# Gate and up projections of two feature blocks at a time: seven products of quarters in place of eight

## The chip, the cores and the metric

The kernel runs on one core of a Trainium2 chip, in one launch. The metric is the device time of that launch in microseconds (us), lower is better. The engines are named as the profile names them: PE (TensorE, matmuls; PEld is its weight load), DVE (VectorE), ACT (ScalarE), POOL (GpSimd) and SP (SyncE, which issues the DMAs here).

## The reference, cut to what matters

A first block, then two layers, each a mixer of four branches followed by a feed-forward part; 512 tokens of width 1024 in float32. Only the feed-forward part of the two layers is changed:

```python
D_MODEL, SEQ, D_FF = 1024, 512, 2816

def hybrid_layer(x, ...):                 # twice, on 512 x 1024
    ...                                   # four branches, merged by gates
    x = x + merged.astype(dt) @ w_out
    h2 = rms_norm(x, norm2_g)
    ffn = (jax.nn.silu(h2 @ w_ffn_gate) * (h2 @ w_ffn_up)) @ w_ffn_down
    return x + ffn
```

## The kernel before

**Split numbers.** Every float32 operand of a matmul is kept as two tiles, a high part (`hi`, a cast on ACT) and the rest (`lo`, a subtraction on POOL, in some places on DVE). One product is three matmuls into the same PSUM bank, high by high, high by low and low by high (`mm3`, lines 246 to 250), each with its own load of 128x128 weights.

**Feed-forward part.** The 2816 features are 22 blocks of 128. `act` holds the normalised tokens, transposed: 8 tiles of 128 features by 512 tokens, `hi` and `lo`. `block` computes one feature block: `proj_t` (line 252) takes the 8 weight tiles of gate, splits them four at a time (`split_w`, line 215: 128x512, cast on ACT at line 220, low part on POOL at line 222, three buffers for each part), and runs 8 x 3 matmuls of 512 columns; `silu2` (line 350) follows, then the same for up, the product (line 1067) and its two parts `yh` and `yl`. `down` multiplies two finished blocks by their rows of `w_ffn_down` (`proj_n`, lines 296 to 298) and adds the result to `x` (`add_resid`, line 497). It runs one block behind, so PE always has work whose operands are there. The last four blocks have no `down` of their own: `proj_resid` (line 543) takes their weights ahead, split into the buffers `pth`, `ptl` and `ks`, and finishes the token tiles one by one, each followed by its norm.

**Edges.** Before the feed-forward part `proj_resid` multiplies by `w_out_2`; per token tile `norm_tile` (line 523) normalises, transposes on PE and splits into `act`. The last of these steps are handed on in `k.late` and run inside the first gate projection, half of the tokens at a time (`proj_late`, lines 267 to 279).

**Order.** PE runs in the order in which the program is written; the other engines' instructions are ordered by a scheduler at build time, each queue then runs strictly in order. Waits between engines come from the tiles: a tile's buffer is given again when its last reader is through. Weight loads go through three buffers `raw` of 128x1024 (512 KB each). `t2` has six buffers, `p` four, PSUM eight banks.

Of the kernel before, what the change touches and what calls it, by code (L numbers as in the profile page):

```python
# [18 lines left out]
P = 128  # L19
S = 512  # L20
# [47 lines left out]
class Task:  # L68
    def __init__(self, gen, cost):
        self.gen, self.left, self.done = gen, cost, False  # L70
# [89 lines left out]
def pe_cost(n):  # L160
    return max(n / 2.4 + 3, 110)
# [3 lines left out]
def hybrid_kernel(ctx: ExitStack, tc: tile.TileContext, i: dict, out: bass.AP):  # L165
# [77 lines left out]

    def mm3(ps, sh, sl, mh, ml, first, last):

        T_.matmul(ps, sh, mh, start=first, stop=False)  # L248
        T_.matmul(ps, sh, ml, start=False, stop=False)  # L249
        T_.matmul(ps, sl, mh, start=False, stop=last)  # L250

    def proj_t(outs, raw, nk):

# [284 lines left out]
    def proj_resid(get, ap, k0, nk, on_tile, delay=1):  # L538

        pss = [[bank(), bank()] for _ in range(NT)]  # L540
        for kk in range(nk - 4):
# [479 lines left out]
def hybrid_layer(k, spill, h, l, last):  # L1021
# [19 lines left out]
    def on_tile(t, pss):  # L1041
        for half, ps in enumerate(pss):
            k.add_resid(x, t, half, ps, ss)
        return k.norm_tile(x[:, t], t, ss, act, gain)

    k.proj_resid(lambda kk, t: tuple(a[:, kk, t * P:(t + 1) * P] for a in act), i["w_out_2"][l], 0, KD, on_tile)
    return ffn(k, x, l, act, last)


def ffn(k, x, l, h, last):  # L1050
    nc, i, new, V, A_, f, pool, bank, stream = k.nc, k.i, k.new, k.V, k.A_, k.f, k.pool, k.bank, k.stream
    gw, uw = (k.w_cols(i[n][l]) for n in ("t_gate", "t_up"))
    wd = i["w_ffn_down_2"][l]

    def get(kk):
        return h[0][:, kk], h[1][:, kk]

    def block(last=False):
        pg = bank()
        for _ in k.proj_t([(pg, get)], next(gw), KD):  # L1060
            pass
        gt = k.silu2(pg, k.t2())
        pu = bank()
        for _ in k.proj_t([(pu, get)], next(uw), KD):
            pass
        pr = k.t2()
        V.scalar_tensor_tensor(pr, pu, 0.5, gt, ALU.mult, ALU.mult)  # L1067
        hi, lo = k.y_tile()
        A_.copy(hi, pr)
        (V if last else k.G).tensor_tensor(lo, pr, f(hi), ALU.subtract)  # L1070
        return hi, lo

    def down(a, acts):
        for half in range(2):
# [18 lines left out]
    ss = new(k.small, [P, 8], "xss")  # L1093
# [16 lines left out]
    k.proj_resid(lambda kk, t: tuple(b[:, t * P:(t + 1) * P] for b in acts[kk]), wd, KF - 4, 4, on_tile)  # L1110
    return (None, None) if last else (spill, h)


# [743 lines left out]
```

## Time and profile before

| | |
|---|---|
| median of 3 runs | 2634.25 us (2632.74 to 2640.15) |
| profiled execution | 2637.59 us, span 2635.8 us |
| mean granted TensorE clock | 0.989 |
| PE busy | 2554.8 us, 97% |
| DVE, ACT, POOL busy | 1334.6, 1162.8, 1291.5 us (51%, 44%, 49%) |

The span runs from the first instruction of the program to the last; the 1.8 us between it and the time of the same execution lie around it. Busy times of different engines overlap, and a matmul counts as busy until its modelled end, so neighbouring matmuls overlap as well. The granted clock is 1.00 at the full 2.4 GHz and 0.50 at 1.2.

### The profile page before, as it was taken

The numbers are of one execution on the slowest core, as the hardware profiler recorded it, in microseconds if no ns is written. First come the engines' busy times: TensorE is split into PE (matmuls) and PEld (weight loads), VectorE is DVE, ScalarE is ACT, GpSimd is POOL, SyncE is SP. The second block draws the span as 40 slices with busy tenths as digits, with TensorE's granted clock in tenths as the row PEclk, the third lists the DMA queues.
The fourth block names the chain that finished last, engine by engine and source line by source line (L and its number), as shares of the span: only waits on it lengthen the run. The fifth ranks groups of instructions, "written<-read, shape, count | busy, mean of one in ns | idle before, by whom it ended". The sixth has DMA issues, their size and how long they took to land.

```text
span 2635.8 us, 36300 instructions
## 1 busy us (share of the span) xinstructions
PE 2554.8 (97%) x12918; PEld 2127.0 (81%) x12918; DVE 1334.6 (51%) x2895; ACT 1162.8 (44%) x2533; POOL 1291.5 (49%) x1112
## 2 busy tenths in 40 slices
PE   7999989999999999999999999999999999999998
PEld 7878778778887887788888887888888877888887
DVE  3677547858536466432222368685364573322223
ACT  4567645436534445332222454365454453322223
POOL 3443345442465543545555555524655535455554
PEclk9999999999999999999999999999999999999999
DMA  4542232222436332422222332223364233222222
GB/s 144 143 130 69 82 125 97 70 77 72 135 112 180 114 104 81 144 81 96 96 96 96 109 110 69 83 73 103 122 182 127 94 91 139 85 96 96 96 96 88
DMA packets 117732, 276.96 MB, mean 105 GB/s; under 512 B 15824, under 2 KB 37584, under 8 KB 117552
## 3 DMA queue, kind: packets, MB, share of 16 engines
q1 hardware_dynamic: 117552, 274.65, 33.2%
q8 instruction: 102, 1.67, 0.3%
q14 instruction: 78, 0.64, 0.1%
HBM read 230.26 MB, written 6.46 MB: 90 GB/s over the span
## 4 chain that ended last, share of the span: by engine, by line
PE 75%; DVE 10%; POOL 4%; issue 4%; DMA 3%; ACT 2%; SPq 0%; POOLq 0%; DVEq 0%; ACTq 0%
PE A L248 17%; PE A L249 16%; PE A L250 16%; PE A L296 5%; PE A L297 5%; PE A L298 5%; PE A L314 4%; PE A L443 3%; POOL wlo L222 2%; DMA raw<-in_w_out_dram 1%; DVE ptl L211 1%; DMA cb<-in_c_rpb_z_dram 1%; PE A L488 1%; DVE sm L331 1%; PE A L278 1%
## 5 line engine op out<-in xcount | busy, mean ns | idle before, releaser
L222 POOL TENSOR_TENSOR wlo<-raw,whi 128x512 fp32r<-128x512 f32 (+2 forms) x721 | 926.7, 1288 | 903.1 <-ACT whi L220 894.8
L220 ACT CAST whi<-raw 128x512 fp32r<-128x512 f32 (+2 forms) x733 | 443.9, 608 | 777.6 <-PE A L249 447.4
L248 PE MATMUL A<-hi,whi 128*128 128x512 f32 (+1 forms) x1848 | 744.3, 403 | 0.4 <-ACT hi L210 0.4
L250 PE MATMUL A<-hi,wlo 128*128 128x512 f32 (+1 forms) x1848 | 725.7, 393 | 10.3 <-DVE wlo L222 5.8
L249 PE MATMUL A<-lo,whi 128*128 128x512 f32 (+1 forms) x1848 | 727.0, 393 | 0.4 <-DVE lo L211 0.4
L250 PEld LDWEIGHTS A<-hi,wlo 128*128 128x128 f32 x1848 | 349.7, 189 | 91.0 <-DVE wlo L222 7.5
L248 PEld LDWEIGHTS A<-hi,whi 128*128 128x128 f32 x1848 | 350.4, 190 | 66.2 <-ACT whi L220 0.9
L249 PEld LDWEIGHTS A<-lo,whi 128*128 128x128 f32 x1848 | 350.3, 190 | 64.2 <-DVE lo L211 0.6
L314 PE MATMUL A<-ident,p 128*128 128x128 f32 (+3 forms) x1125 | 175.5, 278 | 28.1 <-DVE p L527 19.9
L497 DVE TENSOR_TENSOR x<-x,A 128x512 f32<-128x512 f32 x176 | 120.0, 688 | 154.0 <-PE A L298 96.8
L314 PEld LDWEIGHTS A<-ident,p 128*128 128x128 f32 (+3 forms) x1125 | 135.7, 139 | 67.2 <-DVE p L527 19.1
L211 DVE TENSOR_TENSOR ptl<-A,pth 128x512 fp32r<-128x512 f32 (+3 forms) x256 | 148.9, 583 | 80.0 <-ACT pth L210 78.9
L332 ACT ACTIVATE p<-p,sm 128x512 f32<-128x512 f32 (+6 forms) x160 | 100.7, 629 | 155.2 <-DVE sm L331 154.0
L354 DVE SCALAR_TENSOR_TENSOR t<-t,A 128x512 f32<-128x512 f32 x44 | 30.3, 688 | 252.7 <-ACT t L353 252.7
L210 ACT CAST pth<-A 128x512 fp32r<-128x512 f32 (+3 forms) x256 | 127.5, 502 | 54.6 <-PE A L314 54.2
L310 POOL TENSOR_TENSOR rstd<-rstd,mhalf 128x1 f32<-128x1 f32 (+2 forms) x80 | 56.0, 701 | 194.4 <-DVE rstd L309 187.8
L296 PE MATMUL A<-whi,hi 128*128 128x256 f32 (+7 forms) x440 | 145.9, 332 | 0.0
L297 PE MATMUL A<-wlo,hi 128*128 128x256 f32 (+7 forms) x440 | 143.1, 325 | 1.1 <-POOL wlo L222 1.1
L298 PE MATMUL A<-whi,lo 128*128 128x256 f32 (+7 forms) x440 | 142.9, 325 | 0.0
L1067 DVE SCALAR_TENSOR_TENSOR t<-A,t 128x512 f32<-128x512 f32 x44 | 30.4, 692 | 171.2 <-PE A L250 171.2
L296 PE MATMUL A<-whi,yh 128*128 128x512 f32 x288 | 112.1, 389 | 0.0
L297 PE MATMUL A<-wlo,yh 128*128 128x512 f32 x288 | 112.1, 389 | 0.0
(365 smaller groups left out, 4563.3 us busy)
## 6 DMA issues: line engine op xcount, KB each, us to landing
raw<-in_t_gl_dram SPq DMA_DIRECT2D x64, 512.0 KB, 3.5
raw<-in_t_gate_dram SPq DMA_DIRECT2D x44, 512.0 KB, 3.4
raw<-in_t_up_dram SPq DMA_DIRECT2D x44, 512.0 KB, 3.4
raw<-in_w_ffn_down_dram SPq DMA_DIRECT2D x44, 512.0 KB, 3.7
raw<-in_w_in_dram SPq DMA_DIRECT2D x26, 512.0 KB, 3.5
raw<-in_w_out_dram SPq DMA_DIRECT2D x24, 512.0 KB, 3.5
ks<-sth SPq DMA_DIRECT2D x64, 128.0 KB, 2.4
ks<-stl SPq DMA_DIRECT2D x64, 128.0 KB, 2.4
```

The lines of the kernel that those rows point to most:

```text
L210: A_.copy(hi, ps)
L211: V.tensor_tensor(lo, ps, f(hi), ALU.subtract)
L220: A_.copy(hi, src)
L222: (V if k.lo and k.turn % k.lo == 0 else G).tensor_tensor(lo, src, f(hi), ALU.subtract)
L248: T_.matmul(ps, sh, mh, start=first, stop=False)
L249: T_.matmul(ps, sh, ml, start=False, stop=False)
L250: T_.matmul(ps, sl, mh, start=False, stop=last)
L296: T_.matmul(ps, sh, wh[:, j], start=(b + j == 0), stop=False)
L297: T_.matmul(ps, sh, wl[:, j], start=False, stop=False)
L298: T_.matmul(ps, sl, wh[:, j], start=False, stop=(b + j == nk - 1))
L314: T_.transpose(dst, src, ident[0:k, 0:k])
L497: V.tensor_tensor(xx, xx, ps, ALU.add)
```

## The change

Two feature blocks are computed at a time. The 1024 x 256 weights of the two blocks are four quarters (512 features of the input by 128 output features each: a11, a12 of the first block, a21, a22 of the second), the tokens are four quarters too (512 features by 256 tokens: b11, b12, b21, b22), and the result is four quarters of 128 by 256. In place of eight products of quarters, seven are formed, from sums of quarters (Strassen's scheme in Winograd's form). The sums of the weights, s1 to s4, are made per call of `fast_pair`; those of the tokens, t1 to t4, once per layer by `Tokens.sums`, from float32 copies of the token quarters that `norm_tile` now writes as well. Every sum is split into high and low part as other operands are. A product is 12 matmuls of 256 columns. Three of the seven accumulate onto a bank that was read before (`first=False`). The first gate pair of a layer is computed as before (`plain`). `silu2` of the gates and the products with up now read their operand from SBUF (`dst`) in place of PSUM. `down` always takes two blocks and follows a whole pair; the last four blocks go to `proj_resid`, whose odd weight tiles have new homes.

```diff
-    def mm3(ps, sh, sl, mh, ml, first, last):
+    def mm3(ps, sh, sl, mh, ml, first, last, **kw):
...
-    def norm_tile(x, t, ss, dst, gain):
+    def norm_tile(x, t, ss, dst, gain, quarters=None):
...
-                evict_split(ps.rearrange("p (j c) -> p j c", j=4), *(d[:, 4 * half:4 * half + 4, t * P:(t + 1) * P] for d in dst))
+                src = ps.rearrange("p (j c) -> p j c", j=4)
+                evict_split(src, *(d[:, 4 * half:4 * half + 4, t * P:(t + 1) * P] for d in dst))
+                if quarters:
+                    A_.copy(quarters[half][t // 2][:, :, (t % 2) * P:(t % 2 + 1) * P], src)
...
+    class Tokens:
...
+        def sums(self):
+
+            (b11, b12), (b21, b22) = self.q
+            hi = new(pool, [P, 4, 4, 256], "v", F32R, 1)
+            lo = [new(pool, [P, 2, 4, 256], "ks", F32R) for _ in range(2)]
+            self.t = [(hi[:, j], lo[j // 2][:, j % 2]) for j in range(4)]
+            for c in (slice(0, 2), slice(2, 4)):
+                t = [t2().rearrange("p (k c) -> p k c", k=2) for _ in range(4)]
+                V.tensor_tensor(t[0], b12[:, c], b11[:, c], ALU.subtract)
+                V.tensor_tensor(t[1], b22[:, c], t[0], ALU.subtract)
+                G.tensor_tensor(t[2], b22[:, c], b12[:, c], ALU.subtract)
+                V.tensor_tensor(t[3], b21[:, c], t[1], ALU.subtract)
+                for j in (1, 2, 0, 3):
+                    A_.copy(self.t[j][0][:, c], t[j])
+                    (G if j % 2 else V).tensor_tensor(self.t[j][1][:, c], t[j], f(self.t[j][0][:, c]), ALU.subtract)
...
+    def fast_pair(raw1, raw2, tok, dst):
+
+        a11, a12, a21, a22 = raw1[:, 0:4], raw1[:, 4:8], raw2[:, 0:4], raw2[:, 4:8]
...
+        def split(src, eng):
+            hi, lo = (new(pool, [P, 512], t, F32R, 3).rearrange("p (k c) -> p k c", k=4) for t in ("whi", "wlo"))
+            A_.copy(hi, src)
+            eng.tensor_tensor(lo, src, f(hi), ALU.subtract)
+            return hi, lo
+
+        s1, s2, s3, s4 = (part() for _ in range(4))
+        h1, l1 = (new(pool, [P, 4, 256], n, F32R).rearrange("p a b -> p (a b)").rearrange("p (k c) -> p k c", k=KD) for n in ("pth", "ptl"))
+        A_.copy(h1, raw1)
+        G.tensor_tensor(l1, raw1, f(h1), ALU.subtract)
+        V.tensor_tensor(s1, a21, a22, ALU.add)
+        V.tensor_tensor(s2, s1, a11, ALU.subtract)
+        w6 = split(s2, V)
+        V.tensor_tensor(s3, a11, a21, ALU.subtract)
+        w7 = split(s3, G)
+        w5 = split(s1, V)
+        V.tensor_tensor(s4, a12, s2, ALU.subtract)
+        t1, t2_, t3, t4 = tok.t
+        pa, pd, pb, pc = (bank()[:, 0:256] for _ in range(4))
+
+        def product(ps, w, m, first=True):
+
+            for j in range(4):
+                mm3(ps, w[0][:, j], w[1][:, j], m[0][:, j], m[1][:, j], first and j == 0, j == 3, skip_group_check=not first)
+            return 12 * pe_cost(256)
+
+        u, (d1, d2) = t2(), dst
+        q, u2 = u[:, 0:256], u[:, 256:512]
+        yield product(pa, (h1[:, 0:4], l1[:, 0:4]), tok.quarter(0, 0))
+        A_.copy(q, pa)
+        yield product(pd, w6, t2_)
+        V.tensor_tensor(u2, q, pd, ALU.add)
+        yield product(pb, w7, t3)
+        V.tensor_tensor(q, u2, pb, ALU.add)
+        yield product(pc, w5, t1)
+        V.tensor_tensor(d2[:, 256:512], q, pc, ALU.add)
+        yield product(pa, (h1[:, 4:8], l1[:, 4:8]), tok.quarter(1, 0), False)
+        A_.copy(d1[:, 0:256], pa)
+        yield product(pb, split(a22, G), t4, False)
+        V.tensor_tensor(d2[:, 0:256], u2, pb, ALU.add)
+        yield product(pc, split(s4, V), tok.quarter(1, 1), False)
+        V.tensor_tensor(d1[:, 256:512], u2, pc, ALU.add)
+
+    def proj_resid(get, ap, k0, nk, on_tile, delay=1, home=None):
...
-            if kk % 2:
+            if home and kk % 2:
+                wh, wl = home()
+            elif kk % 2:
...
-    def block(last=False):
-        pg = bank()
-        for _ in k.proj_t([(pg, get)], next(gw), KD):
+    def plain(w):
+        ps = bank()
+        for _ in k.proj_t([(ps, get)], next(w), KD):
             pass
...
+    def pair(first, last):
+
+        if first:
+
+            gts = [k.silu2(plain(gw), k.t2()) for _ in range(2)]
+            tok.sums()
+        else:
+            gts = [k.silu2(g, k.t2()) for g in fast(gw)]
+        out = []
+        for u, gt in zip(fast(uw), gts):
+            V.scalar_tensor_tensor(gt, u, 0.5, gt, ALU.mult, ALU.mult)
+            hi, lo = k.y_tile()
+            A_.copy(hi, gt)
+            (V if last else k.G).tensor_tensor(lo, gt, f(hi), ALU.subtract)
+            out.append((hi, lo))
+        return out
...
-    for a, n in [(a, 2) for a in range(0, KF - 4, 2)] + [(KF - 4, 4)]:
-        acts = []
-        for j in range(n):
-            acts.append(block(j == 3))
-            if pending:
-                down(*pending)
-                pending = None
+    for a in range(0, KF, 2):
+        acts = pair(a == 0, a == KF - 2)
+        if a == KF - 2:
+            acts = pending[1] + acts
+        elif pending:
+            down(*pending)
         pending = (a, acts)
```

## Rows read from the trace of the kernel before

**Rows 1.** The page, part 1: busy us, share of span, instructions.

```profile
PE 2554.8 (97%) x12918; PEld 2127.0 (81%) x12918; DVE 1334.6 (51%) x2895; ACT 1162.8 (44%) x2533; POOL 1291.5 (49%) x1112
```

**Rows 2.** The page, part 4: chain that ended last, by line.

```profile
PE A L248 17%; PE A L249 16%; PE A L250 16%; PE A L296 5%; PE A L297 5%; PE A L298 5%; PE A L314 4%; PE A L443 3%; POOL wlo L222 2%; DMA raw<-in_w_out_dram 1%; DVE ptl L211 1%; DMA cb<-in_c_rpb_z_dram 1%; PE A L488 1%; DVE sm L331 1%; PE A L278 1%
```

**Rows 3.** Windows, both layers: us, busy PE PEld DVE ACT POOL, clock, DMA.

```profile
1200.00:1300.00 100.00, 100.00 (x436) 81.55 (x436) 24.95 (x37) 29.33 (x49) 54.33 (x43) 1.00 0.28 95
...
2400.00:2500.00 100.00, 100.00 (x436) 81.55 (x435) 25.19 (x38) 29.08 (x48) 54.65 (x43) 1.00 0.28 95
```

**Rows 4.** Timeline of PE, first layer: start us, us, engine, line, operation.

```profile
1160.70 0.40 PE L248 MATMUL A<-hi,whi 128*128 128x512 f32 x1
...
1163.48 0.40 PE L296 MATMUL A<-whi,yh 128*128 128x512 f32 x1
...
1174.38 0.40 PE L248 MATMUL A<-hi,whi 128*128 128x512 f32 x1
```

**Rows 5.** Timeline of PE: first and last of 96 matmuls, 256 columns.

```profile
396.70 0.28 PE L296 MATMUL A<-whi,hi 128*128 128x256 f32 x1
...
407.90 0.28 PE L298 MATMUL A<-whi,lo 128*128 128x256 f32 x1
```

**Rows 6.** Groups: PEld 396:408, POOL and ACT 1200:1300 (busy, mean ns | idle).

```profile
L296 PEld LDWEIGHTS A<-whi,hi 128*128 128x128 f32 x32 | 6.0, 188 | 0.0
...
L222 POOL TENSOR_TENSOR wlo<-raw,whi 128x512 fp32r<-128x512 f32 x37 | 47.9, 1294 | 45.8 <-ACT whi L220 45.8
L220 ACT CAST whi<-raw 128x512 fp32r<-128x512 f32 x37 | 23.0, 621 | 69.7 <-PE A L249 45.3 <-PE A L298 24.4
```

**Rows 7.** Groups by line and form, DVE, whole span.

```profile
L497 DVE TENSOR_TENSOR x<-x,A 128x512 f32<-128x512 f32 x176 | 120.0, 688 | 154.0 <-PE A L298 96.8 <-PE A L250 57.2
...
L211 DVE TENSOR_TENSOR v<-A,v 128x256 fp32r<-128x256 f32 x24 | 9.2, 417 | 4.0 <-ACT v L210 3.9
...
L1468 DVE TENSOR_TENSOR t<-t,t 128x512 f32<-128x512 f32 x10 | 6.9, 688 | 0.2
```

**Rows 8.** Groups by form: POOL and ACT at 256 columns, whole span.

```profile
L1631 POOL TENSOR_TENSOR cb<-cb,cst 128x256 f32<-128x256 f32 x32 | 24.2, 762 | 29.0 <-DMA cb<-in_c_rpb_z_dram 22.1 <-PE A L250 2.6 <-DVE ptl L211 1.8
...
L210 ACT CAST v<-A 128x256 fp32r<-128x256 f32 x24 | 8.5, 373 | 3.3 <-PE A L298 3.0
```

**Rows 9.** Timeline: a DVE operation behind a POOL operation.

```profile
1060.88 1.29 POOL L222 TENSOR_TENSOR wlo<-raw,whi 128x512 fp32r<-128x512 f32 x1 [1.45 <-ACT whi L220]
...
1061.07 1.64 DVE L1152 TENSOR_TENSOR x<-x,t 128x512 f32<-128x512 f32 x1
```

**Rows 10.** Timeline of DVE and POOL: the same at 547 us.

```profile
547.34 1.29 POOL L222 TENSOR_TENSOR wlo<-raw,whi 128x512 fp32r<-128x512 f32 x1
...
547.40 1.77 DVE L1463 TENSOR_TENSOR t<-t,rstd 128x512 f32<-128x512 f32 x1 [1.76 <-POOL rstd L310]
```

**Rows 11.** Timeline of ACT, feed-forward part of the first layer.

```profile
1144.05 0.62 ACT L220 CAST whi<-raw 128x512 fp32r<-128x512 f32 x1 [1.26 <-PE A L249]
...
1147.35 0.59 ACT L353 ACTIVATE t<-A 128x512 f32<-128x512 f32 x1
```

**Rows 12.** Timeline, start of that part: ACT's last casts, PE's next matmul.

```profile
1132.13 1.31 ACT L210 CAST hi<-A 128x512 fp32r<-128x512 f32 x2 [2.63 <-PE A L314]
...
1135.69 0.39 PE L248 MATMUL A<-hi,whi 128*128 128x512 f32 x1
```

**Rows 13.** Timeline of PE behind idle; that window, columns as in rows 3.

```profile
537.05 0.33 PE L314 MATMUL A<-ident,yn 128*128 128x128 f32 x1 [1.75 <-DVE yn L1384]
...
537.75 0.42 PE L297 MATMUL A<-wlo,hi 128*128 128x256 f32 x1
...
540.74 0.41 PE L296 MATMUL A<-whi,hi 128*128 128x256 f32 x1
...
537.00:541.00 4.00, 3.95 (x21) 3.95 (x22) 1.04 (x2) 1.50 (x3) 2.10 (x2) 0.58 0.02 4
```

**Rows 14.** The page, part 6: DMA issues, KB each, us to landing.

```profile
raw<-in_t_gate_dram SPq DMA_DIRECT2D x44, 512.0 KB, 3.4
```

More of the change, by code (lines that the diff above doesn't have):

```diff
@@ L242, in w_cols @@
                 yield raw[:, m]
-    def mm3(ps, sh, sl, mh, ml, first, last):
-        T_.matmul(ps, sh, mh, start=first, stop=False)
-        T_.matmul(ps, sh, ml, start=False, stop=False)
-        T_.matmul(ps, sl, mh, start=False, stop=last)
+    def mm3(ps, sh, sl, mh, ml, first, last, **kw):
+        T_.matmul(ps, sh, mh, start=first, stop=False, **kw)
+        T_.matmul(ps, sh, ml, start=False, stop=False, **kw)
+        T_.matmul(ps, sl, mh, start=False, stop=last, **kw)
     def proj_t(outs, raw, nk):
@@ new lines, in norm_tile, with __init__, quarter @@
+        return second
+    class Tokens:
+        def __init__(self, h, quarters):
+            self.h, self.q = h, quarters
+        def sums(self):
[12 more added lines that the diff above has]
+                    (G if j % 2 else V).tensor_tensor(self.t[j][1][:, c], t[j], f(self.t[j][0][:, c]), ALU.subtract)
+        def quarter(self, a, b):
+            return tuple(z[:, 4 * a:4 * a + 4, 256 * b:256 * b + 256] for z in self.h)
@@ new lines, in fast_pair, with part @@
+    def fast_pair(raw1, raw2, tok, dst):
+        a11, a12, a21, a22 = raw1[:, 0:4], raw1[:, 4:8], raw2[:, 0:4], raw2[:, 4:8]
+        def part():
+            return p_tile().rearrange("p (k c) -> p k c", k=4)
+        def split(src, eng):
[36 more added lines that the diff above has]
+        V.tensor_tensor(d1[:, 256:512], u2, pc, ALU.add)
@@ L1043, in on_tile, with ffn @@
             k.add_resid(x, t, half, ps, ss)
-        return k.norm_tile(x[:, t], t, ss, act, gain)
+        return k.norm_tile(x[:, t], t, ss, act, gain, quarters)
+    quarters = [[a.rearrange("p a b -> p (a b)")[:, 0:1024].rearrange("p (k c) -> p k c", k=4) for a in z]
+                for z in ([k.q_stack().bitcast(F32) for _ in range(2)], [new(k.mix, [P, 2, S], "cst", bufs=2) for _ in range(2)])]
     k.proj_resid(lambda kk, t: tuple(a[:, kk, t * P:(t + 1) * P] for a in act), i["w_out_2"][l], 0, KD, on_tile)
-    return ffn(k, x, l, act, last)
-def ffn(k, x, l, h, last):
+    return ffn(k, x, l, act, quarters, last)
+def ffn(k, x, l, h, quarters, last):
     nc, i, new, V, A_, f, pool, bank, stream = k.nc, k.i, k.new, k.V, k.A_, k.f, k.pool, k.bank, k.stream
     gw, uw = (k.w_cols(i[n][l]) for n in ("t_gate", "t_up"))
+    tok = k.Tokens(h, quarters)
     wd = i["w_ffn_down_2"][l]
@@ L1056, in get, with fast @@
         return h[0][:, kk], h[1][:, kk]
-    def block(last=False):
-        pg = bank()
-        for _ in k.proj_t([(pg, get)], next(gw), KD):
-            pass
-        gt = k.silu2(pg, k.t2())
-        pu = bank()
-        for _ in k.proj_t([(pu, get)], next(uw), KD):
-            pass
[L1066 to L1071, printed above, removed]
+    def plain(w):
+        ps = bank()
+        for _ in k.proj_t([(ps, get)], next(w), KD):
+            pass
+        return ps
+    def fast(w):
+        dst = [k.t2() for _ in range(2)]
+        for _ in k.fast_pair(next(w), next(w), tok, dst):
+            pass
+        return dst
+    def pair(first, last):
[12 more added lines that the diff above has]
+        return out
     def down(a, acts):
@@ L1108, in on_tile, with home @@
             nc.sync.dma_start(k.out[t * P:(t + 1) * P, sl], x[:, t, sl])
-    k.proj_resid(lambda kk, t: tuple(b[:, t * P:(t + 1) * P] for b in acts[kk]), wd, KF - 4, 4, on_tile)
+    homes = iter(((pool, "qs"), (k.mix, "cst")))
+    def home():
+        where, tag = next(homes)
+        return tuple(new(where, [P, 1024], tag, F32R, 2) for _ in range(2))
+    k.proj_resid(lambda kk, t: tuple(b[:, t * P:(t + 1) * P] for b in acts[kk]), wd, KF - 4, 4, on_tile, home=home)
     return (None, None) if last else (spill, h)
```

1 line of the change is left out of this document (removed).

## Prediction

> **What bounds the kernel now.** I read the page first: TensorE (PE) is busy 97% of the span, no other engine above 51% [rows 1], and the largest lines of the chain that ended last are the three matmuls of `mm3`, 49% of the span together [rows 2]. A busy PE only means that matmuls overlap, so the feed-forward part needs a closer look. Windows of 100 us inside that part show PE busy throughout at full granted clock, 436 matmuls each, DVE at 25, ACT at 29 and POOL at 54 [rows 3]. The four that lie there, two in each layer, agree: the stage has no stall, and only fewer or shorter matmuls shorten it. The timeline gives the spacing: 12 projection matmuls of 512 columns from 1160.70 to 1163.48 us, 231.7 ns each; 48 of the down projection from there to 1174.38, 227.1 ns each [rows 4]. Two feature blocks of gate or up are 48 matmuls, 11.12 us.
>
> **The change, term by term.** `fast_pair` stands for 48 matmuls of 512 columns and issues 7 products x 12 = 84 of 256 columns, each with its own weight load. Is half the width half the time? In 396 to 408 us the trace has 96 such matmuls in a row, a fresh weight load for each: 396.70 to 407.90 in 95 steps, 117.9 ns [rows 5]. A load lasts 188 ns [rows 6], longer than that step, so loads overlap each other too, and the weights do not become the limit. One call is 84 x 0.1179 = 9.90 us against 11.12: 1.22 us saved. The first gate pair of a layer stays plain, so a layer has 11 pairs x 2 - 1 = 21 calls, two layers 42: **-51.1 us**. The down projection keeps its 24 matmuls per block.
>
> What is added goes to the other engines. Per call: DVE seven 128x512 operations with both inputs in SBUF (s1 to s4, three low parts) and five 256-column additions from PSUM; ACT a 1024-column cast, five of 512 and two 256-column copies out of PSUM; POOL the 1024-column low part of raw1 (`l1`) and two of 512 (w7, a22). Prices are 0.69 and 0.42 us on DVE [rows 7], 0.62 and 0.37 on ACT, 1.29 on POOL for 512 columns [rows 6, 8]. No row has POOL at 1024; from 0.76 at 256 columns [rows 8] to 1.29 at 512 the slope is 0.53 per 256, so 2.36 (lower bound one 512 operation, 1.29; upper two, 2.58; a line through two rows is nearer to the upper). PE needs 2 x 9.90 + 48 x 0.2271 = 30.7 us for a pair (gate, up, down). In that time ACT has 2 x (7 x 0.62 + 2 x 0.37) for the calls and 8 x 0.62 beside (tanh, `yh`, down splits), 15 us. DVE has 14 x 0.69 + 10 x 0.42 + four more with two SBUF inputs (the two of `silu2`, whose source now lies in SBUF, and the two products of gate and up) x 0.69 + 8 additions to x at 0.69 = 22 us. POOL has 2 x (2.36 + 2 x 1.29) + 2 `yl` and 4 down splits at 1.29 = 17.6 us. By that count all is hidden.
>
> But DVE and POOL do not run freely beside each other. An addition on DVE with both inputs in SBUF took 1.64 us where a POOL operation had begun 0.19 us before: POOL ended at 1062.17, DVE at 1062.71 [rows 9]. Another took 1.77 and again ended 0.54 us after a POOL operation that had begun first (549.17 against 548.63) [rows 10]; undisturbed ones take 0.69 [rows 7]. So they take turns, and DVE holds its turn for 0.54. (The Trainium skill, SBUF — State Buffer, section Who interferes with whom, has this as a lock on a shared port pair, held for the whole instruction against a DVE operation with two SBUF inputs; the trace agrees, with the 0.54 us above. Free overlap, the first sum, would give 2587; under the lock the added work has to queue.) DVE additions with one PSUM input stay at 0.69 while POOL works in 54 of 100 us [rows 3, 7] and do not queue. Turns in one pair: POOL 17.6, DVE 18 x 0.54 = 9.7, together 27.3 of 30.7 us. That is 89% full, and PE waits whenever a low part comes late.
>
> How late? The split pool keeps its three buffers. The fourth split of a call (a22) takes the buffer of the first (w6), free when product 2 ends; its low part is wanted by the third matmul of product 6, 3 x 1.415 + 0.24 = 4.48 us on. Cast 0.62 and POOL 1.29 leave 2.6, less some 0.4 of hand-overs: 2.2 us of slack. w7 and the first two down splits have about the same; the low parts made on DVE 2.8. If `l1` (2.36) has just begun and a DVE turn (0.54) comes between, a22 starts 2.90 late and PE stands 0.70 us. Each call has one `l1` and two such splits; with the worst meeting about half the time I take 0.35 per call, **+14.7 us**. Bounds: 0, if nothing meets, and 2.0 (another POOL operation of 1.29 in front as well), +84. The value is nearer to 0 since today POOL waits for ACT and ACT for PE in this stage, never PE for them [rows 3, 6].
>
> Does the text's order matter? In `fast_pair` the cast of a22 stands behind the copy of pa, which waits for product 5, and DVE's low part of s4 behind an addition that waits for product 6. If the queues kept that order, PE would wait 0.37 + 0.62 + 1.29 and 0.42 + 0.69, 3.4 us per call. They do not: at 1144.05 ACT casts weights of up, and only at 1147.35 comes the tanh of the gate, which is written ahead of them [rows 11]. PE alone follows the text. I cost this at nothing.
>
> Edges of the stage, per layer. (a) `norm_tile` adds two 128x512 ACT copies between casts that PE waits for, at 1132.13 to 1133.44 us [rows 12]: 0.4 (0 to 1.1). (b) `Tokens.sums` can start when these casts and copies are through, about 1134.5. It has 6 POOL and 10 DVE turns: 6 x 1.29 + 10 x 0.54 = 13.1. With the last gate split, w7 and a22 (3.9) and the low parts of w6 and w5 (1.1) the turns are taken until 1152.6. PE ends the plain gates at 1135.69 [rows 12] + 24 x 0.2317 = 1141.2 and wants a22 and t4 five products later, at 1148.3. That is 4.3 late; I take 4.0, some of it being movable ahead (0 to 6). (c) The last pair has no down projection beside it, and the eight splits of the tail (10.3 of POOL) fall on it: two calls 17.4, `silu2` and products 2.2, low parts 1.1, altogether 31 of turns against 23.9 of PE until the last of them is wanted (two calls and 18 matmuls), of which some 4.5 (one `l1` and four sums) can go ahead: 2.5 (0 to 5). (d) Where PE stands long its clock halves: after 1.75 us of idle the clock granted over 537 to 541 was 0.58, and 256-column matmuls went from 0.118 to 0.214 us a step (14 steps from 537.75 to 540.74), 1.4 us lost [rows 13]. One such stretch per layer and a little over, 1.7 (0 to 3.4). Together 8.6 x 2 = **+17.2 us**.
>
> Costed at nothing: PSUM reuse (pa, pb and pc are written again two or three products, 2.8 us, after the read of 0.42 begins; without that cover 0.42 per product); weight traffic (the same 512 KB loads, 3.4 us to landing [rows 14], six in 30.7 us through three buffers; on SP's queue the two loads of down stand behind those of up and the next gate's behind them, so if raw2, held until a22 is split, came free a pair late, 3.4 us once per pair).
>
> **Sum.** 2637.6 (the profiled execution) - 51.1 + 14.7 + 17.2 = 2618.4. The median of the runs shown is 3.3 lower, so **2615 us**.
>
> **Rivals.** *All hidden*: the turns interleave and PE stays at 100%: 2637.6 - 51.1 + 1 = 2587, 2584 on the median's scale. For it: 11% of the time no turn is taken and the order adapts. Against: two splits per call with 2.2 us of slack, and an operation of 2.36 that they can meet. *The turns eat it*, the change doing nothing for the time: at 0.81 us of waiting per call ((51.1 - 17.2) / 42) the gain is gone; waits of 0.65 to 1.0 give 2627 to 2642. It comes so if time is lost at each hand-over; DVE ending 0.54 after POOL, no later than its own work needs, speaks against much loss [rows 9, 10]. *Slower*: queues settled beforehand on undisturbed durations put DVE's sums for the next call ahead of low parts that PE needs; from 0.81 us per call on the kernel is slower, and at the upper bound of 2.0 it takes 2637.6 - 51.1 + 84 + 17.2 = 2688. For it: DVE would be at 72% before any waiting. Against: every product leaves at least 2.2 us. That 256-column matmuls fall back to 131 ns or more, where 84 cost as much as 48 now, is excluded by [rows 5] unless the clock falls.
>
> **Numbers.** My forecast (2597 to 2626) 0.42, all hidden 0.20, eaten 0.18, slower 0.20. A change under 0.3% (8 us) can't be told from none. Faster 0.62, same 0.18, slower 0.20. The range, 2588 to 2652, leaves out the best part of all hidden and the worst half of slower.
>
> **What the profile after should show.** Some 84 x 42 matmuls of 256 columns at 118 ns start to start where PE does not wait; PE busy below 100% in the middle of the feed-forward part, its idle time in front of `wlo` matmuls and released by POOL; DVE operations with two SBUF inputs above 0.69 us in the mean, one with PSUM unchanged; PE waits of a few us where the up products of the first pair begin, and some at the tail. Wrong would be: no PE waits at all (then 2584), waits on PSUM additions or on DMA, or half clock through the stage.

## The result and the profile after

The changed kernel takes **2742.5 us** (median of 4 runs, 2737.7 to 2752.5) against 2635.2 for the kernel before: ratio **1.041** (95% interval 1.038 to 1.044). It is slower by 107 us, far outside the predicted range. The profiled execution took 2742.57 us with a span of 2740.8, 105.0 longer than before's.

First the page, part 1, of the kernel after, to be held against [rows 1], then windows over the two feed-forward stages (from the last `proj_late` of a layer to the next, or to the end) of before and of after, columns as in [rows 3].

```profile
PE 2553.2 (93%) x14430; PEld 2194.7 (80%) x14430; DVE 1705.8 (62%) x3421; ACT 1269.7 (46%) x2733; POOL 1333.8 (49%) x1080
```

```profile
1128.00:1499.30 371.30, 369.83 (x1643) 301.83 (x1641) 97.26 (x150) 115.54 (x201) 199.42 (x157) 1.00 0.29 99
2260.90:2628.40 367.50, 366.95 (x1619) 299.42 (x1617) 95.30 (x146) 111.73 (x193) 195.07 (x154) 1.00 0.28 95
```

```profile
1131.70:1554.00 422.30, 368.08 (x2400) 335.72 (x2397) 283.20 (x413) 165.41 (x296) 218.55 (x141) 0.95 0.27 87
2317.30:2733.80 416.50, 365.83 (x2375) 332.57 (x2373) 282.07 (x409) 162.12 (x288) 215.03 (x138) 0.95 0.27 84
```

Read the two pairs from left to right. The stages grew by 51.0 and 49.0 us, 100 of the 105: nothing else moved much. PE, which had next to no idle time there (1.5 and 0.5 us), now has 54.2 and 50.7 (length less busy time): 102.9 more. PE's busy time hardly fell, although its matmuls are shorter; the clock column says why. At a mean of 0.95 some 5% of 838.8 us, 42, was lost to the lower clock. What is left, 100.0 - 102.9 - 42 = -45 us, is the saving: by this remainder it came, near the predicted 51. Waiting and the lower clock around the waits took it three times over.

What PE waited for in the whole span (us in total, times, longest), largest first:

```profile
PE A L250 <- POOL wlo L580: 53.9, 20, 3.1
...
PE A L297 <- POOL wlo L222: 18.7, 20, 1.9
PE A L248 <- ACT v L564: 18.2, 4, 5.4
```

L250 is the third matmul of `mm3`, L580 the low part inside `split`. Twenty waits are one for each of the 20 gate calls that `fast_pair` makes, 2.7 us each. L564 is the cast of the token sums, at the start of each stage. One pair, in the middle of layer 0, shows how the long wait arises. PE at the wait (start, length, [idle before]), and then the clock of the stretches around it (windows, columns as above):

```profile
1319.08 0.39 PE L250 MATMUL A<-v,wlo 128*128 128x256 f32 x1 [2.88 <-POOL wlo L580]
...
1320.43 0.41 PE L248 MATMUL A<-v,whi 128*128 128x256 f32 x1
...
1323.63 0.30 PE L248 MATMUL A<-hi,pth 128*128 128x256 f32 x1
```

```profile
1319.00:1320.00 1.00, 0.93 (x7) 0.93 (x8) 0.91 (x2) 0.00 (x0) 1.00 (x2) 1.00 0.00 0
1320.50:1323.50 3.00, 3.00 (x16) 3.00 (x16) 2.86 (x6) 1.06 (x2) 0.22 (x1) 0.50 0.40 149
```

This wait costs 2.88 us and then once more: from 1320.5 to 1323.5 the granted clock is 0.50, the 1.2 GHz level, and a step of 256 columns takes 0.21 us (15 from 1320.43 to 1323.63) in place of 0.118. Not every wait is paid twice like this one: of the 20, 12 came with such a stretch, and 38 of the 85 us at half clock lie at the two starts and at the end of layer 0. Now backwards from the wait: POOL, ACT, DVE and SP's DMA issues before it (each a timeline, the last the line's own view: first and last start).

```profile
1314.94 2.39 POOL L586 TENSOR_TENSOR ptl<-raw,pth 128x1024 fp32r<-128x1024 f32 x1 [4.66 <-ACT pth L585]
1317.28 1.75 POOL L580 TENSOR_TENSOR wlo<-p,whi 128x512 fp32r<-128x512 f32 x1
```

```profile
1312.22 0.62 ACT L579 CAST whi<-p 128x512 fp32r<-128x512 f32 x1 [6.84 <-DVE p L588]
1313.81 1.05 ACT L585 CAST pth<-raw 128x1024 fp32r<-128x1024 f32 x1 [0.97 <-DMA raw<-in_t_up_dram]
```

```profile
1308.41 0.71 DVE L587 TENSOR_TENSOR p<-raw 128x512 f32<-128x512 f32 x1 [4.71 <-DMA raw<-in_t_gate_dram]
1309.05 2.47 DVE L497 TENSOR_TENSOR x<-x,A 128x512 f32<-128x512 f32 x4
1311.44 0.68 DVE L588 TENSOR_TENSOR p<-p,raw 128x512 f32<-128x512 f32 x1
```

```profile
L240 SPq DMA_DIRECT2D raw<-in_t_gate_dram x2: 340/340/340, 1296.0 to 1304.9; - x2
```

The gate call's first load is issued at 1296.0, its second only at 1304.9: it had to wait for one of the three raw buffers, which the down projection's splits give back. So `s1` (L587) starts at 1308.41, four additions into x stand between it and `s2` (L588), and the first cast is made at 1312.22. Then the queues: ACT casts `h1` of the *up* call (L585) before the gate's w7, and POOL makes `l1` of the up call (L586, 2.39 us) before w7's low part, which PE is waiting for. Three candidate causes lie in one picture: late weights, the fixed order of the queues, and the turns of DVE and POOL (the 1.75 us of the low part, 1.29 undisturbed [rows 6]).

### The profile page after: what moved, and what is told of

Same layout as the page of the kernel before. It is cut to its first block, busy times and chain, and to the rows that moved or that the text cites. A ratio compares the mean times of both kernels' runs of the same rounds, so it can differ in the third digit from the quotient of the medians.

```text
span 2740.8 us, 40242 instructions
## 1 busy us (share of the span) xinstructions
PE 2553.2 (93%) x14430; PEld 2194.7 (80%) x14430; DVE 1705.8 (62%) x3421; ACT 1269.7 (46%) x2733; POOL 1333.8 (49%) x1080
## 4 chain that ended last, share of the span: by engine, by line
PE 55%; DVE 12%; POOL 12%; DMA 9%; issue 8%; ACT 4%; SPq 0%; POOLq 0%; DVEq 0%; ACTq 0%
PE A L250 12%; PE A L248 12%; PE A L249 12%; POOL wlo L222 4%; PE A L314 4%; DMA raw<-in_t_gate_dram 4%; PE A L443 3%; PE A L297 2%; PE A L296 2%; PE A L298 2%; POOL wlo L580 2%; DMA raw<-in_t_up_dram 2%; POOL ptl L586 1%; POOL yl L1170 1%; DMA raw<-in_w_out_dram 1%
## 5 line engine op out<-in xcount | busy, mean ns | idle before, releaser
L222 POOL TENSOR_TENSOR wlo<-raw,whi 128x512 fp32r<-128x512 f32 (+4 forms) x553 | 718.5, 1304 | 643.1 <-ACT whi L220 637.9
L248 PE MATMUL A<-hi,whi 128*128 128x512 f32 (+2 forms) x1344 | 526.9, 392 | 0.4 <-ACT hi L210 0.4
L250 PE MATMUL A<-hi,wlo 128*128 128x512 f32 (+2 forms) x1344 | 508.6, 378 | 10.3 <-DVE wlo L222 5.8
L249 PE MATMUL A<-lo,whi 128*128 128x512 f32 (+2 forms) x1344 | 508.2, 378 | 0.4 <-DVE lo L211 0.4
L220 ACT CAST whi<-raw 128x512 fp32r<-128x512 f32 (+4 forms) x565 | 338.5, 604 | 349.5 <-PE A L249 164.4
L250 PEld LDWEIGHTS A<-hi,wlo 128*128 128x128 f32 x1344 | 255.2, 190 | 62.4 <-DVE wlo L222 7.5
L250 PE MATMUL A<-v,wlo 128*128 128x256 f32 x672 | 202.8, 302 | 57.3 <-POOL wlo L580 53.9
L248 PE MATMUL A<-v,whi 128*128 128x256 f32 x672 | 199.5, 297 | 19.7 <-ACT v L564 18.2
L249 PE MATMUL A<-ks,whi 128*128 128x256 f32 x672 | 199.0, 296 | 4.4 <-POOL ks L565 4.4
L250 PEld LDWEIGHTS A<-v,wlo 128*128 128x128 f32 x672 | 137.0, 204 | 63.3 <-POOL wlo L580 58.4
L586 POOL TENSOR_TENSOR ptl<-raw,pth 128x1024 fp32r<-128x1024 f32 x42 | 103.1, 2456 | 144.5 <-ACT pth L585 138.4
L248 PEld LDWEIGHTS A<-v,whi 128*128 128x128 f32 x672 | 136.0, 202 | 21.5 <-ACT v L564 19.2
```

What stands on the lines that cost most here:

```text
L220: A_.copy(hi, src)
L222: (V if k.lo and k.turn % k.lo == 0 else G).tensor_tensor(lo, src, f(hi), ALU.subtract)
L248: T_.matmul(ps, sh, mh, start=first, stop=False, **kw)
L249: T_.matmul(ps, sh, ml, start=False, stop=False, **kw)
L250: T_.matmul(ps, sl, mh, start=False, stop=last, **kw)
L586: G.tensor_tensor(l1, raw1, f(h1), ALU.subtract)
```

## Experiments

For each run: its time, PE's idle time in the two stages together, and how long the granted clock was 0.5 in them (from the trace as above; before has 2.0 and 0 us). Times are one run each; those of after, best2, best5, best7, best9 and best10 are medians of 4 to 12.

| run | us | idle | half clock |
|---|---|---|---|
| after | 2742.5 | 104.9 | 85 |
| order_l1 | 2739.4 | 97 | 79 |
| gate_bufs | 2704.5 | 79 | 41 |
| order_gate | 2696.8 | 81 | 41 |
| no_sums | 2737.8 | 104 | 89 |
| w7_dve | 2721.2 | 92 | 51 |
| up_only | 2665.8 | 36 | 38 |
| evict | 2705.8 | 80 | 48 |
| best1_raw | 2711.1 | 76 | 65 |
| best1 | 2654.6 | 39 | 38 |
| best2 | 2651.8 | 36 | 20 |
| best5 | 2635.7 | 28 | 3 |
| best7 | 2634.4 | 26 | 0 |
| best9 | 2636.4 | 30 | 3 |
| best10 | 2625.1 | 27 | 0 |

**Order alone (order_l1).** `k.behind` holds the cast and low part of a22 of the call before.

```diff
-        A_.copy(h1, raw1)
-        G.tensor_tensor(l1, raw1, f(h1), ALU.subtract)
+        with ExitStack() as held:
+            for ins in k.behind:
+                held.enter_context(tc.issue_after(ins.ins))
+            A_.copy(h1, raw1)
+            G.tensor_tensor(l1, raw1, f(h1), ALU.subtract)
```

> The cast h1 and low part l1 of each Strassen call are put, in the queues of ACT and POOL, behind the casts and low parts of the call before, so that POOL's order per pair becomes w7 (gate), a22 (gate), l1 (up) instead of l1 (up), w7, a22. The queue-order theory (l1 of 2.4 us stands ahead of the low part that product 3 waits for; the wait of some 2.7 us per pair then also costs a half-clock stretch of some 1.6 us): 20 gate calls lose the wait and most of the clock loss, about 2742 - 54 - 20 = 2667 us, and the idle time at product 3 falls from 54 us to under 10. The theory that the exclusive turns of DVE and POOL are the cost: about 2730 us, the wait moves to another product. The late-weights theory (the gate call's second load comes too late, whatever stands in the queues): 2720 us or more.

2739.4 us: the order changed as meant and next to nothing came of it. The wait at product 3 is gone, with the loads as late as before, and one of the same size stands elsewhere. PE's waits of this run, then DVE and POOL of one pair:

```profile
PE A L248 <- DVE t L615: 42.3, 16, 2.8
```

```profile
1316.94 1.50 DVE L592 TENSOR_TENSOR p<-raw 128x512 f32<-128x512 f32 x1 [0.21 <-DMA raw<-in_t_up_dram]
1318.53 2.70 DVE L593 TENSOR_TENSOR p<-p,raw 128x512 f32<-128x512 f32 x1
1321.15 0.68 DVE L595 TENSOR_TENSOR p<-raw,raw 128x512 f32<-128x512 f32 x1
...
1322.26 0.42 DVE L615 TENSOR_TENSOR t<-t,A 128x256 f32<-128x256 f32 x1
```

```profile
1317.85 2.83 POOL L591 TENSOR_TENSOR ptl<-raw,pth 128x1024 fp32r<-128x1024 f32 x1
```

L615 reads pb, which product 6 writes next. In DVE's queue `s1`, `s2` and `s3` of the *up* call stand ahead of it; `s1` waits for the up weights' load, `s2` for its turn behind `l1`. `l1` ends at 1320.68, `s2` at 1321.23, 0.55 later, as in [rows 9, 10]: 2.0 of the 2.8 us are this one turn (2.70 us in place of 0.69). The queue-order theory in its first form, one misplaced `l1`, is refuted; a wider one (work of the next call ahead of what PE needs, on each of three engines) is not.

**Wider buffers alone (gate_bufs).** From the second pair on the gate weights use two buffers of their own.

```diff
-    gw, uw = (k.w_cols(i[n][l]) for n in ("t_gate", "t_up"))
+    def loads(ap):
+        for a in range(ap.shape[0]):
+            raw = k.raw_tile() if a < 2 else new(k.mix, [P, 1024], "cst", bufs=2)
+            raw = raw.rearrange("p (k c) -> p k c", k=KD)
+            nc.sync.dma_start(raw, ap[a, :, 0])
+            yield raw
+    gw, uw = loads(i["t_gate"][l]), k.w_cols(i["t_up"][l])
```

> From the second pair of blocks on, the gate weights have two buffers of their own, so that the second gate load no longer waits until the down projection's splits have given back one of three raw buffers. The late-weights theory (s1 to s3 start 2 to 5 us late because the load lands late): the wait at the gate call's product 3 goes, about 2667 us. The queue-order theory: the load lands early and the sums start earlier, but l1 of the up call still stands ahead of w7's low part in POOL's queue and itself needs the up weights and its own turn, so the time depends on whether that order changes; with the order as it was, 2715 to 2742 us. The turns theory: about 2730 us.

2704.5 us, 38 less: about half of what the late-weights theory had forecast. The wait at product 3 is gone, half of the half-clock time too. PE's waits now:

```profile
PE A L297 <- POOL wlo L222: 28.3, 20, 1.8
PE A L248 <- DVE t L612: 20.9, 18, 1.2
```

The buffers changed the order as well. POOL's queue, from the gate's w7 of one pair to the down projection:

```profile
1307.34 1.29 POOL L580 TENSOR_TENSOR wlo<-p,whi 128x512 fp32r<-128x512 f32 x1 [0.92 <-ACT whi L579]
...
1332.33 2.43 POOL L586 TENSOR_TENSOR ptl<-raw,pth 128x1024 fp32r<-128x1024 f32 x1 [3.73 <-ACT pth L585]
1334.71 2.51 POOL L222 TENSOR_TENSOR wlo<-raw,whi 128x512 fp32r<-128x512 f32 x2
```

The gate's w7 is made before its call begins at 1309.14, and an up call's `l1` no longer stands in front of it but in front of the down projection's low parts, for which PE waits instead (28.3 us). So the 38 us are those of early weights and a new order together.

**Without three sums (no_sums).**

```diff
-        V.tensor_tensor(s1, a21, a22, ALU.add)
-        V.tensor_tensor(s2, s1, a11, ALU.subtract)
+        s1, s2, s3 = a21, a11, a22
...
-        V.tensor_tensor(s3, a11, a21, ALU.subtract)
```

> The three sums s1, s2, s3 of weight quarters are left out (the quarters a21, a11, a22 are used in their place; s4 and all splits, products and token sums stay), so the output is not the reference's: this leaves out 3 of 4 DVE operations of some 0.6 us for each of 42 calls and the chain through them. The turns theory (DVE's sums and POOL's low parts shut each other out): 2690 us or less. The queue-order theory: casts and low parts stand in the same queues, l1 (up) still ahead of w7 (gate), so 2700 us or more. The late-weights theory: the casts still need the second load, so 2715 us or more.

2737.8 us. DVE is relieved by a quarter (the window beside that of after, where DVE had 70.46 in the same 100 us), and nothing is won that can be told: the four runs of the changed kernel lie between 2737.7 and 2752.5. The wait at product 3 stayed (52.9 us): the turns of these three sums are not what it came from.

```profile
1200.00:1300.00 100.00, 89.35 (x612) 83.56 (x612) 51.83 (x84) 39.48 (x68) 48.58 (x31) 0.95 0.28 90
```

**w7's low part on DVE (w7_dve).**

```diff
-        w7 = split(s3, G)
+        w7 = split(s3, V)
```

> w7's low part is computed on DVE in place of POOL (so POOL keeps l1 and a22 of a call, DVE has w6, w7, w5, s4). The queue-order theory: the low part that product 3 waits for no longer stands behind l1 on POOL; the wait of 54 us in all at product 3 falls to under 20 and the time to about 2680 us, if DVE does not have something of its own ahead of it. The turns theory: DVE's low part has to take its turn against the same l1 all the same (POOL holds the turn for some 2.4 us), so 2720 us or more. The late-weights theory: 2720 us or more.

2721.2 us, just inside the 2720 or more of two theories, and far above the 2680 that the queue-order theory set on condition that DVE has nothing of its own ahead. POOL's wait at product 3 became one for DVE (40.1 us in 39 waits of at most 2.0), and the half-clock time fell from 85 to 51 us. It moves the wait and shortens it; it does not tell the turns from the late weights.

**Order and buffers (order_gate)**: both diffs above.

> Both edits together: the gate weights have their own two buffers from the second pair on, and h1 and l1 of each Strassen call are queued behind the casts and low parts of the call before. The wider buffers alone gave 2704.5 us and the order alone 2739.4, against 2742.5 with neither. If the order was a second, independent cause that the late weights had masked, the two together give 2685 us or less, the wait of 20.9 us for the eviction of product 4 by DVE goes and only the 28 us at the down projection's low part are left. If only the late load counted, 2700 to 2710 us. If what is left is the turns of DVE and POOL, it moves between products and the time stays within 10 us of 2704.

2696.8 us, only 8 less than the buffers alone: within the 10 us of 2704 that the turns theory had forecast, and not the 2685 of a second cause. What is left is the wait for the read of pc by DVE (L617; 55.1 us in 36 waits): 0.4 us in each gate call and 2.6 in each up call. DVE and POOL ahead of one of the long ones, then PE:

```profile
2420.07 2.80 DVE L580 TENSOR_TENSOR wlo<-p,whi 128x512 fp32r<-128x512 f32 x1 [1.02 <-ACT whi L579]
2422.90 1.64 DVE L598 TENSOR_TENSOR p<-cst,p 128x512 f32<-128x512 f32 x1
2424.46 0.41 DVE L617 TENSOR_TENSOR t<-t,A 128x256 f32<-128x256 f32 x1
```

```profile
2419.89 2.42 POOL L591 TENSOR_TENSOR ptl<-cst,pth 128x1024 fp32r<-128x1024 f32 x1
```

```profile
2425.02 0.35 PE L248 MATMUL A<-hi,whi 128*128 128x256 f32 x1 [2.61 <-DVE t L617]
```

A low part of the up call takes 2.80 us in place of 0.69, since the next gate call's `l1` had begun on POOL just before, and the next gate call's s4 (L598) stands behind it, also for longer than 0.69. These two turns, 2.1 and 0.95 us over, are more than the whole 2.6: here the turns do set the wait, by what the order puts side by side.

**Up alone (up_only).** The gate stays plain: `gts = [k.silu2(plain(gw), k.t2()) for _ in range(2)]` in all pairs.

> The gate projection stays plain throughout; only the up projections go by seven products (22 calls). By the decomposition of the changed kernel's trace the up calls themselves hardly wait: 22 x 1.22 = 27 us are saved, and the ends of the stage stay (two starts of 11 us of waits and 7 of half clock, the end of layer 0 with 5): 2637 - 27 + 41 = about 2650 us. The late-weights theory: the gate's plain call splits its raw quarter as it comes, no sum of two loads is waited for, so no wait of 2 us or more is left in the steady part: 2650 us as well. The turns theory: each call still costs 0.8 us or more, so 2660 us or more.

2665.8 us: above the 2650 of two theories, within the turns theory's 2660 or more, but not for its reason. In the middle PE is busy 98% at full clock; the waits left there are some 0.5 us per pair, at a plain gate call's low part on POOL (9.8 us in 18 waits). Yet the run is 32 us slower than the kernel before on the same chip (2633.3): 36 us of idle time and half of 38 us at the low clock are more than the 27 us saved (27 - 36 - 19 = -28, which is what the two stages of the profiled runs differ by; the time outside them is the same, and the remaining 4 us are those between two runs of the kernel before). The largest wait in the stages is at the starts, for the token sums (5.9 us per layer). The starts are a cost of their own.

**Three waits treated one by one (evict)**: wider buffers and

```diff
-        V.tensor_tensor(d2[:, 256:512], q, pc, ALU.add)
+        A_.copy(d2[:, 256:512], pc)
+        V.tensor_tensor(d2[:, 256:512], q, d2[:, 256:512], ALU.add)
...
-        for u, gt in zip(fast(uw), gts):
+        for u, gt in zip([plain(uw) for _ in range(2)] if first else fast(uw), gts):
...
-            A_.copy(hi, gt)
+            (V.tensor_copy if last else A_.copy)(hi, gt)
```

> The gate weights' own buffers, and three edits of what was still waited for with them: the first pair's up projections are plain too, so that the token sums are needed 20 us later; the partial result of product 4 is evicted by ACT (a copy) before DVE adds it; in the last pair the cast of the activations is on DVE in place of ACT. If each wait seen in the run with the wider buffers alone (2704.5 us) is a cause by itself, their removal gives: two starts with 7.8 us of waits and some 7 of half clock, less 2.4 for two plain calls, 27; evictions 20.9; end of layer 0 4.6 and 2 of half clock: 2704.5 - 27 - 21 - 6 = 2650 us. If the waits in the steady part only move on (to the next low part or sum that has to take its turn), 2670 us or more.

2705.8 us: nothing won over gate_bufs, against a forecast of 2650 (2670 or more if the waits move on). DVE's wait vanished and POOL's at the down projection grew from 28.3 to 47.4 us: the waits move on.

**All of it with the full order (best1).** Evict's edits, and `h1` and `l1` are queued behind every split before them in the text, the down projection's too (`k.behind = cast, low` also in `split_w`). **The same through three raw buffers (best1_raw).**

> All of the edits together: the gate weights' own buffers, plain up projections in the first pair, product 4 evicted by ACT, the last pair's cast on DVE, and h1 and l1 of each call queued behind the casts and low parts of the split before it in the text, the down projection's among them. The queue-order theory: the down projection's wait for POOL (28 us) goes as well, 2650 - 28 - some 5 of clock = about 2617 us, faster than before the change. The turns theory: what is left of waits per pair stays at 1 us or more, so 2645 us or more.

> As the run with all edits together (2654.6 us), but the gate weights come through the three raw buffers again. If the late second load is a cause of its own, which no order of the queues cures, most of the 38 us that the wider buffers gave alone come back: 2690 us or more, with DVE's sums waiting for the load in each pair. If the order of the queues (h1 and l1 ahead of the splits of the call before, the down projection's too) was the whole cause: 2670 us or less.

2654.6 us with the buffers, 2711.1 without. The window of best1 in the middle:

```profile
2400.00:2500.00 100.00, 98.27 (x672) 90.82 (x671) 90.00 (x114) 44.97 (x81) 65.83 (x40) 1.00 0.31 98
```

PE at 98% and full clock, DVE at 90% and POOL at 66% at once: taking turns does not by itself prevent it. Three runs share the three edits of evict: with the buffers alone 2705.8, with the full order alone 2711.1, with both 2654.6. **Either cause alone keeps PE waiting: with the other one mended, the order is worth 51 us and the buffers 56.** In the two stages alone, by the traces, it is 52 and 49 (best1_raw ran on another chip, where the kernel before took 2640). Evict and best1 have the same operations on DVE and POOL; what differs is which stand behind which. In after, the buffers with the order that came with them had brought 38. Forecast 2617 for best1 was missed mainly by the two starts (a wait of 5.3 for `h1`, then 2.0 and 1.0, and 13.7 us of half clock, in each layer): `cst` holds token quarters until the sums are made, so the second pair's load came late.

**Starts and ends (best2, best5, best7).** best2: the second pair's loads through the raw buffers (`a < 4`) and the last pair's up projections plain. best5: the second pair's gate plain too, and each `split_w` queued behind the split before. best7: at the end, every other slice's low part on DVE:

```diff
-                G.tensor_tensor(wl[:, sl], raw[:, sl], f(wh[:, sl]), ALU.subtract)
+                (V if home and kk % 2 else G).tensor_tensor(wl[:, sl], raw[:, sl], f(wh[:, sl]), ALU.subtract)
```

> As the run with all edits together (2654.6 us), but the second pair's gate loads use the raw buffers (its buffers hold token quarters until the token sums are made), and the last pair's up projections are plain too. In that run each start still had 8.6 us of waits and a half-clock stretch of 13.7 us (6.9 lost), the end of layer 0 had 4 and 3. If these are what keeps it above the kernel before: 2654.6 - 2 x 15.5 - 5 + 2.4 = about 2621 us, ratio 0.995, faster than before. If the token sums' own work on DVE, POOL and ACT keeps the start late whatever buffers it has, 2640 us or more, not faster.

> As the run before with product 4 evicted by ACT, the orders and plain edges (2645.1 us profiled, ratio 1.004), with two edits: the second pair's gate projections are plain too, so that the token sums are first needed some 10 us later, and every split's cast and low part is queued behind the split before it in the text. In that run each start had 6.5 to 7 us of waits for product 2's cast, 1 to 1.4 behind it and a half-clock stretch of 7 to 10 us. If the start was late only because the token sums and the weight sums share DVE in those 10 us: 2 x (8 + 4) - 2 x 1.2 for the plain calls = 21 us less, about 2624 us, ratio 0.995 or less. If the sums only move the wait to the next call, no change: 1.002 to 1.006.

> As the run beside it, with one edit more: at the end of the stage the low parts of every other of the last four down-projection slices are on DVE in place of POOL. In the run before, POOL's low part of product 3 in the last gate call came 1.1 to 2.7 us late and the following two 0.7 to 2.1, behind the slices' low parts of 2.5 us each pair. If POOL's queue at the end is the cause: 2 x (4 + 1.5) = 11 us less than beside it, about 2613 us. If the turns of DVE and POOL are, within 3 us of it.

Ratios 1.0039 (1.0023 to 1.0055), 0.9990 (0.9977 to 1.0003) and 0.9993 (0.9982 to 1.0004). best2 missed its 0.995: the start waited 6.8 us for w6's cast instead, since `s2` stood behind the token sums on DVE, of which most took 1.2 to 2.9 us in place of 0.69: there the turns do count. best5 took 13 us off it by the ratios (0.0049 x 2637), of 21 expected; its half-clock time in the stages is 3 us. best7 won 1 us of the 11 expected, within what can be told: POOL's queue at the end was not worth what I took it for.

**The turns once more (best9, best10).** best9: `l1` as two POOL instructions of 512 elements. best10: also all of the token sums on DVE (`G` and the choice of `G` or `V` in `Tokens.sums` become `V`).

> As the run with every other slice's low parts on DVE (2634.4 us, ratio 0.9993), with l1 in two POOL instructions of 512 elements in place of one of 1024. There, every third pair had 1.7 us of waits in the second call (DVE's sum s3 had taken 2.77 us, waiting for its turn behind an l1 of 2.84). If the turns set these: the waits at DVE's low part and eviction fall from 6.8 us per layer to under 2, 2634 - 2 x 5 - some 2 = about 2622 us. If they are set by DVE's load alone or POOL's second instruction costs as much turn time: 2632 us or more.

> As the run beside it, and the token sums are made by DVE alone (POOL's 12 operations of the two layers that DVE has to take turns with are moved to DVE). At the start, POOL's low parts of the second pair's plain gate calls came 1.7 and 1.6 us late behind POOL's part of the sums. If POOL's queue there is the cause: 2 x 3.3 and about 2 of what follows each wait less than beside it, about 2613 us; faster than the kernel before by 0.8%. If DVE, which then has all 14 operations of each layer's sums, is late in its place: no change or slower than beside it.

best9 is no faster than best7 (0.9991, 0.9980 to 1.0002): the long waits in every third pair became 0.85 us in each pair, and DVE still waits out two shorter holds. best10: **0.9944 (0.9929 to 0.9960)**, 2625.1 us, faster than both kernels. Its two stages, and two of its waits (the first is the only one from 1200 to 1400 us):

```profile
1121.60:1486.30 364.70, 351.27 (x2291) 318.67 (x2290) 300.16 (x389) 163.49 (x301) 222.88 (x152) 1.00 0.32 101
2249.10:2611.30 362.20, 348.95 (x2267) 316.13 (x2265) 295.24 (x384) 159.56 (x293) 218.88 (x149) 1.00 0.30 97
```

```profile
PE A L254 <- DVE wlo L584: 13.7, 16, 0.9
PE A L254 <- POOL wlo L225: 13.0, 9, 2.2
```

Both stages are shorter than before's, by 6.6 and 5.3 us. So 12 us are what the change itself brings at last. The profiled runs of best9 and best10 differ by 12 us, 5 of them in the stages; outside, where DVE, ACT and POOL have the same operations in the same order, the other 7 are the clock: 52 us at half clock there in best9 and 37 in best10 (before has 59). Why it differs there, and whether it does so in the other runs, is not shown.

## Why the prediction was wrong

**The saving was right.** 84 matmuls of 256 columns cost what [rows 5] said, wherever PE did not wait. 45 us were saved of 51.1, by a remainder that has the rounding of the clock column in it (about 4 us). Some of the rest may be the step behind each wait: in the pair shown PE's next matmul starts at 1319.30, 0.22 us behind the one that waited.

**The step that failed: "weight traffic" costed at nothing.** I wrote that if raw2 came free a pair late it would cost 3.4 us once per pair, and left that at zero because loads land in 3.4 us [rows 14]. The change needs two loads before its first sum, where a plain call starts with one. The trace shows the second load issued 8.9 us behind the first, and a wait of 2.7 us per pair at PE, 53.9 us in all. The late load is a condition of that wait and not its only cause (order_l1 removed it too); with the order mended, early weights are worth 49 to 56 us.

**"Does the text's order matter?" was costed at nothing too.** The queues do adapt, as [rows 11] showed, but once, beforehand. I named this as the mechanism of *Slower* (work for the next call ahead of what PE needs) and gave it 0.20. It is what order_l1's DVE queue shows, and the pair evict and best1 prices it at 51 us once the weights are early. "Against: every product leaves at least 2.2 us" was the error: that slack counts from the moment at which a buffer comes free, and the work began several us after that moment.

**The turns** were the term I had worked out most carefully: +14.7 by 0.35 us per call. The mechanism is there: DVE's `s1` took 1.39 us in the mean, and additions with one PSUM input were unchanged.

```profile
L497 DVE TENSOR_TENSOR x<-x,A 128x512 f32<-128x512 f32 x176 | 110.5, 676 | 57.5 <-PE A L250 57.5
...
L587 DVE TENSOR_TENSOR p<-raw 128x512 f32<-128x512 f32 x42 | 58.5, 1393 | 101.7 <-DMA raw<-in_t_gate_dram 101.3
```

(The Trainium skill, SBUF — State Buffer, section Who interferes with whom, has such an operation wait until the other engine's instruction is through; `s2` in order_l1 did, ending 0.55 us behind `l1`.) But a count of turns, 27.3 of 30.7 us, did not find what was late: no_sums takes three of them from each call and gains at most 5 us. A turn counts where it falls in front of what PE needs: 2.0 of the 2.8 us in order_l1, the whole 2.6 in order_gate. So the turns are a part of the cause and not refuted: their forecasts of the time held in order_gate, up_only, evict and best1, and failed in gate_bufs (about 2730) and no_sums (2690 or less). Where weights and order were mended, best10 has 0.85 us per pair, 0.43 per call; that this is close to the 0.35 is partly luck, since the 0.35 was for two splits on POOL and the wait is at a low part on DVE.

**Edges.** For the token sums I took 4.0 us per layer and 6 at most; the waits for L564 and for the sums' low parts were 9.1 + 2.2. I let the sums start at 1134.5; `Tokens.sums` began on DVE at 1149.3, behind `silu2` and `s1`, `s2` of the next call, one of them waiting for its load. Again the order. The end cost 4.6 in layer 0 (forecast 2.5).

**The clock.** I took one half-clock stretch per layer, 1.7 us. There were stretches at 12 of the 20 waits at product 3 (44 us at half clock), at the two starts and the end of layer 0 (38) and at one other wait (3): 85 us, of which half, 42, is lost. This term alone is more than the 37 us from the forecast to the top of the range. That *half clock through the stage* was listed as a sign against the forecast was right; it was not in the price of *Slower*, which is why that rival too ended at 2688. With the waits shown (102.9), the clock (42) and the saving (-45) the sum is 2637.6 + 100 + 5 outside the stages; it closes because the saving is the remainder.

**What stays open**: the 5 us outside the stages (4 of them are idle time of PE), the clock outside them, why a wait of one size brought the low clock in one run and not in another, how the 105 us divide between weights, order and turns, and why best7's edit at the end gave so little. A fourth raw buffer for all loads, in place of the gate's own two, was not tried.

## What to carry to other kernels

Work that is hidden by its sum over a cycle is hidden only if it *starts* in time: for each added operation, ask when its last input lands, and follow the load's issue back to the buffer that it needs. In a kernel whose queues are ordered beforehand, ask for each engine what of the *next* call stands ahead of the operation that PE waits for, or takes its turn in front of it; curing one of several such causes moves the wait and gains less than its share, so try cures in pairs before dropping one, and look whether a cure has changed the order too. And look at the clock beside the waits: here it cost 42 us on top of 103, but by no fixed rate per wait.

## What the runs showed of the hardware

- A wait of some 2.6 us does not bring the low clock by its size alone. A stretch at 0.50 came with 12 of the 20 waits at product 3 in after (1.5 to 3.1 us), 11 of 18 of 2.3 to 2.8 us in best1_raw, 3 of 18 of 2.4 to 2.7 in evict, and none of 17 of 2.6 to 2.8 in order_gate. Order_gate's window below has three of these (one is the PE line shown with that run) and is at 1.00. What decides it is not shown.

```profile
2400.00:2500.00 100.00, 91.01 (x638) 84.65 (x638) 78.79 (x106) 41.35 (x71) 55.28 (x36) 1.00 0.30 95
```

- The low clock need not begin with the wait's end: in the pair shown PE ran at full clock from 1319.08 to past 1320.0 and then fell. At the end of layer 0 it fell at 1528.5, within a wait that lasted from 1524.6 to 1529.2.
- A POOL operation of 1024 columns took 2.39 us in the pair shown (estimated 2.36), so the line through two shorter ones [rows 8] held.
